# Strassen feed-forward: input tiles of 128 rows, sums on VectorE, five plain blocks, one pair's steps last with second buffers

## The chip, the cores and the metric

The kernel runs on one core of a Trainium2 chip. The metric is the device time of one execution in microseconds (us). TensorE (PE in the profile) multiplies, VectorE (DVE) and ScalarE (ACT) do element-wise work, GpSimd (POOL) too, and SyncE (SP) issues the transfers (DMA). Each engine works through its own queue in order.

## The reference, cut to what matters

One step of an encoder layer for 1104 rows (64 sample rows, 16 meta rows, 1024 prompt rows). The change touches only the first of its two feed-forward blocks:

```python
def half_ffn(x, g, wg, wu, wd):          # x: 1104 x 1024, wg, wu: 1024 x 2816, wd: 2816 x 1024
    h = rmsnorm(x, g)
    return x + 0.5 * ((jax.nn.silu(h @ wg) * (h @ wu)) @ wd)
```

Afterwards come the mixing heads, attention and a second feed-forward block of the same form, which the diff leaves as they are.

## The kernel before

**Numbers.** Every fp32 factor is split into a high part (ScalarE cast to fp32r) and a low part (VectorE: source minus high part), and every product takes three passes on TensorE (`PASSES`, `mm3`): high·high, high·low, low·high.

**Strassen steps.** The 1104 columns of the transposed input are four groups c of F = 276 columns; groups 0 and 1 are pair p = 0, groups 2 and 3 pair p = 1. Of each pair the four quarters (group × upper or lower half of the 1024 features) and sums of them give seven operands, split in `norm_pair`. The 2816 inner columns are 22 blocks j of 128. For a block and a pair, `half_steps` makes gate and up products with seven operand products (`STEPS`) of 12 matmuls, 84 in all; `plain_steps` makes the same without Strassen with 96. Both write the gated result to DRAM (`hd`).

**Weights.** `seq` lists the steps; each step e has a weight set: `half_loads` loads 1 MB in three transfers (`rA` the gate block, `rL` and `rH` the halves of the up block), `half_weights` and `last_weights` form the sums and split them into rings of buffers (`A`, `S`, `T`, `B`). Before, `seq` is 7 blocks for pair 0 alone (two of them plain), the same 7 for pair 1 alone, 13 blocks for both pairs at once (j = 7 to 19), and blocks 20 and 21 for pair 0 and then for pair 1: 31 weight sets. A step for one pair is called a single here, one for both a double. Four sums per Strassen set run on GpSimd (`G.tensor_tensor`); raw buffers `rA`, `rL`, `rT` and split buffers `S`, `T`, `B` exist once, `A` and `rH` twice.

**Input.** `in_rows` brings x in as 12 tiles of 92 rows (three per column group), turns them with TensorE transposes and copies them to `st` and `s` tiles; `norm_pair` scales them; `spill` stores the turned input (`x0`). The vectors of norms and convolutions come in `start2`.

**Down projection.** `down` multiplies with `wd` in groups of two blocks; `down_loads` prepares `wd`, `inner_loads` reads `hd` back and splits it; `x4` are four rows of `x0` for its first residual sums. `first_pair_done` opens their buffers when pair 0 has been used for the last time.

**Order.** A planner (`Tasks`, with the model times of `Clock`) writes out the order of every engine's queue at build time: among tasks whose planned inputs are there, the lowest rank goes first. On the chip the queues then run in this order, whatever arrives late. All DMA of this stage go through SP's one queue. All instructions carry line 424 (a helper), so the profile is read by tiles: `bk` is a PSUM bank, `s` and `st` input tiles, `wx`, `wh`, `wl`, `raw` weight buffers, `sn` and `hb` the results on their way out.

Of the kernel before, what the change touches and what calls it, by code (L numbers as in the profile page):

```python
# [17 lines left out]
P = 128  # L18
# [675 lines left out]
FT = [(0, 92), (92, 92), (184, 92)]  # L694
# [24 lines left out]
def in_rows(s, c, gi, src, xr, dst, ss, fl, rank, before=(), after=()):  # L719

    nc, T = s.nc, s.tasks
    lo, n = FT[gi]
    yield (0, *before)
    xr = xr().rearrange("p k t -> p (k t)")[:, :DM]
    for r0, nr, ap in src:
        nc.sync.dma_start(xr[r0:r0 + nr], ap)
    yield (nc.lag(xr), *after)

    def squares(out):
        nc.scalar.activation(out[:n], xr[:n], AF.Square, accum_out=ss[:n, 3 * (c % 2) + gi:3 * (c % 2) + gi + 1])  # L730
        fl.add((c, gi), nc.complete(ss))
    if c < 2:
        squares(s.waste)
    for h in range(2):
        yield 0, "b"
        b = grab(s)
        for k in range(4):
            nc.tensor.transpose(b[:, k * P:k * P + n], xr[:n, (4 * h + k) * P:(4 * h + k + 1) * P], s.ident[:n, :n])
        T.add(in_out(s, dst(h)[:, :, lo:lo + n], b, n, h, lambda h=h: fl.add((c, gi, h))), rank)
    if c > 1:  # L740
        yield
        squares(xr)
    fl.add(("xr", c, gi))


def in_out(s, dst, b, n, h, done):
    nc = s.nc
    (nc.scalar.copy if h else nc.vector.tensor_copy)(dst, b.rearrange("p (k t) -> p k t", k=4)[:, :, :n])
# [6 lines left out]
def norm_pair(s, p, ss, src, x, raw, more, gain, wk, waits, ready, spill):  # L755
# [3 lines left out]
    V, G = nc.vector, nc.gpsimd  # L759
    raws = None  # L760

    def low(eng, i, src, tile=None):
        x.low(eng, i, src, tile)
        ready.add((p, i), nc.complete(x.l[i]))
    for i in (0, 1):
# [3 lines left out]
        rsqrt(s, wk, r, ss[:, 3 * i:3 * i + 3], P, 3, 1.0 / DM, EPS)  # L769
# [6 lines left out]
        for gi, (lo, n) in enumerate(FT):  # L776
            nc.tensor.matmul(rb[:, lo:lo + n], s.ones, dg[:, gi, :n], start=True, stop=True)
# [3 lines left out]
        for h in (0, 1):  # L781
# [14 lines left out]
    X3, X4 = x.new(13), x.new(5)  # L796
# [32 lines left out]


# [10 lines left out]

def half_weights(s, seq, rings, raw, W):

    nc, T = s.nc, s.tasks
    V, G, A = nc.vector, nc.gpsimd, nc.scalar

    def split(names, srcs, dst, raws):
        h, l = dst
        for i, (n, x) in enumerate(zip(names, srcs)):
            A.copy(h[:, 512 * i:512 * i + 512], x)  # L850
        yield nc.lag(h)
        for i, (n, x) in enumerate(zip(names, srcs)):
            o = slice(512 * i, 512 * i + 512)
            V.tensor_tensor(l[:, o], x, f32(h[:, o]), ALU.subtract)
            W[e, n] = h[:, o], l[:, o]
        T.free(*raws)
    for e in (0, 1):
        to = rings["ST"[e]]
# [14 lines left out]
    for e in range(2, len(seq)):  # L873
# [4 lines left out]
        G.tensor_tensor(t0, a0, b0, ALU.subtract)  # L878
# [5 lines left out]
        G.tensor_tensor(b0, b0, b1, ALU.add)  # L884
# [4 lines left out]
        G.tensor_tensor(a0, b0, a0, ALU.subtract)  # L889
        yield nc.lag(a0), "S"  # L890
        yield from split(("S0", "S1"), (b0, a0), rings["S"].take(), ("rL",))
        G.tensor_tensor(a1, a1, a0, ALU.subtract)
        yield nc.lag(a1), "T"
        yield from split(("T0", "T1"), (t0, a1), rings["T"].take(), ("rT", "rA"))


def last_weights(s, seq, rings, raw, W):

    nc, T = s.nc, s.tasks
    for e in range(2, len(seq)):  # L900
# [9 lines left out]
def plain_steps(s, js, W, x, ready, tmp, hd, done):  # L910
# [22 lines left out]
    for c in (0, 1):  # L933
        for e in (0, 1):
            bs = []
            for n in "AB":
                yield 0, "b", nc.when(W, (e, n))
                b = grab(s)
                for k in range(8):
                    op = (0, 1, 7, 2)[2 * c + k // 4]  # L940
                    if k % 4 == 0:
                        yield 0, ready.wait((0, op))
                    mm3(nc, b[:, :F], [w[:, k * P:k * P + P] for w in W[e, n]], (x.h[op][:, k % 4, :], x.l[op][:, k % 4, :]), k == 0, k == 7)
                bs.append(b)
                if n == "A":
                    T.add(gated(e, c, bs), -1)
            if c:
                T.free("A", "ST"[e])


def half_steps(s, seq, W, x, ready, tmp, hd, done, hooks):
# [25 lines left out]
    for e, (j, ps) in list(enumerate(seq))[2:]:  # L977
        bs, sn, hbs, fl = {}, {}, {}, Flags()
        for name, op, i, bk in STEPS:
# [31 lines left out]
            if op in last:  # L1011
                T.free(last[op])
# [4 lines left out]
def down_loads(s, wd, slots, W):  # L1017

    nc, T = s.nc, s.tasks
    raws = []  # L1020
# [6 lines left out]
    yield from load(0)  # L1027
    for j in range(NF):
        if j + 1 < NF:
# [9 lines left out]
        T.free("raw")  # L1039
# [1172 lines left out]
def layer_kernel(tc, cst, x_prompt, x_sample, cache_mla_ckv, cache_mla_krope, state_gdn, state_conv, meta,  # L2212
# [21 lines left out]
    with ExitStack() as ctx:  # L2234
# [46 lines left out]
        ss = [wk.tile([P, 6], F32, name=f"ss{p}") for p in (0, 1)]  # L2281
        for x in ss:
            nc.vector.memset(x, 1.0)
# [4 lines left out]
        def half_of(c, h):  # L2288
            if c < 2:
                return stage[c][:, 4 * h:4 * h + 4, :]  # L2290
            if (c, h) not in staged:
                staged[c, h] = x01[1].new({(2, 0): 9, (2, 1): 10, (3, 0): 12, (3, 1): 13}[c, h])
            return staged[c, h]

        def rows_of(o, n):
            out = []
            for a, b, ap in ((0, NS, x_sample[0]), (NS, NS + NM, meta), (NS + NM, T_, x_prompt[0])):
                lo, hi = max(a, o), min(b, o + n)
                if lo < hi:
                    out.append((lo - o, hi - lo, ap[lo - a:hi - a, :]))  # L2300
            return out
        xr = [2, 3, 4, 5, 6, 8, 11]
        for c in range(4):
            for gi, (o, n) in enumerate(FT):
                i = 3 * c + gi
                T.add(in_rows(s, c, gi, rows_of(F * c + o, n), lambda i=i: x01[1].new(xr[i % 7]), lambda h, c=c: half_of(c, h), ss[c // 2], tin, -4 if c < 2 else 8,
                              (tin.wait(("xr", (i - 7) // 3, (i - 7) % 3)),) if i > 6 else (), (n1.wait((0, 0)),) if c > 1 else ()), -3 if c < 1 else -1.5 if c < 2 else 10 + i)

        def there(c, h=None):
            return tin.wait(*[(c, gi) if h is None else (c, gi, h) for gi in range(3)])  # L2310
# [47 lines left out]
        state_px, x4 = {}, []  # L2358
# [260 lines left out]
```

## Time and profile before

| | us |
|---|---|
| median of 3 runs | 2513.24 (2512.9 to 2514.95) |
| profiled execution | 2513.59 |
| its span | 2511.8 |
| PE busy in the span | 2379.2 (95%) |
| DVE, ACT, POOL busy | 1371.3, 824.3, 453.7 |

The span is what the trace covers; 1.8 us of the execution lie outside it. Forty slices of the span show PE at 5 to 8 tenths in the first slices and at 9 or more in nearly all the others. Busy PE is modelled, and matmuls overlap, so the mean duration of one matmul is longer than the distance between two of them.

### The profile page before, as it was taken

The page shows a single profiled execution, that of the slowest core. Times are in us where ns is not written, and L with a number is a line of the kernel's source. Part 1 is how long each engine was busy: PE and PEld are TensorE (multiplying, and loading weights), DVE is VectorE, ACT ScalarE, POOL GpSimd, SP SyncE. Part 2 cuts the span into 40 slices and gives each one's busy share as a digit, 9 for nine tenths or more (in the row PEclk, how much of TensorE's full clock was granted, in tenths as well). Part 3 has the DMA queues.
Part 4 walks back from the last instruction along what each step waited for, and adds up shares of the span by engine and source line. Part 5 has one row for each costly group of instructions (what it writes and reads, how often), then busy time and mean ns, then how long its engine had stood idle before and what let it go on. Part 6 is the DMA issues. An engine that isn't in the chain of part 4 may idle for free.

```text
span 2511.8 us, 39219 instructions
## 1 busy us (share of the span) xinstructions
PE 2379.2 (95%) x15552; PEld 2344.1 (93%) x15552; DVE 1371.3 (55%) x3105; ACT 824.3 (33%) x1847; POOL 453.7 (18%) x679
## 2 busy tenths in 40 slices
PE   5868999998999999989998999999999999999999
PEld 5767999998999989989998999999999999999998
DVE  3776644445666666778877656634333333233335
ACT  4343433333111245455543555423111111111113
POOL 0454422222000041332236200221000000000002
PEclk6889999999999999999998999999999999999999
DMA  4323322226322133111122102621111111111011
GB/s 139 105 69 92 97 74 78 78 77 207 120 88 96 39 103 95 37 55 45 53 63 73 53 15 76 209 59 54 48 34 34 51 51 51 42 43 43 27 41 72
DMA packets 210944, 181.28 MB, mean 72 GB/s; under 512 B 12748, under 2 KB 192120, under 8 KB 210632
## 3 DMA queue, kind: packets, MB, share of 16 engines
q1 hardware_dynamic: 210744, 178.77, 23.3%
q8 instruction: 122, 2.00, 0.3%
q14 instruction: 62, 0.51, 0.1%
q10 hardware_dynamic: 16, 0.00, 0.0%
HBM read 143.14 MB, written 35.60 MB: 71 GB/s over the span
## 4 chain that ended last, share of the span: by engine, by line
PE 77%; DVE 9%; DMA 5%; POOL 3%; issue 3%; ACT 2%; SPq 1%; DVEq 0%; POOLq 0%; ACTq 0%
PE bk L424 77%; DMA raw<-in_ffn_wu_dram 2%; DVE wl L424 1%; DMA wx<-in_ffn_wg_dram 1%; DVE cv L424 1%; DVE s L424 1%; POOL raw L424 1%; ACT wh L424 1%; DVE wx L424 1%; SPq L424 1%; DVE rs_q L424 1%; DMA raw<-in_w_out_dram 1%; DMA s<-in_x_prompt_dram 1%; DVE rs_r L424 0%; POOL wx L424 0%
## 5 line engine op out<-in xcount | busy, mean ns | idle before, releaser
L424 PE MATMUL bk<-XH,wh 128*128 128x384 f32 (+1 forms) x1264 | 354.4, 341 | 0.0
L424 PE MATMUL bk<-XL,wh 128*128 128x384 f32 (+1 forms) x1264 | 349.2, 337 | 1.4 <-POOL XL L424 0.8
L424 PE MATMUL bk<-XH,wl 128*128 128x384 f32 (+1 forms) x1264 | 348.5, 336 | 0.0
L424 ACT CAST wh<-raw 128x1024 fp32r<-128x1024 f32 (+5 forms) x124 | 115.0, 928 | 661.4 <-PE bk L424 601.0
L424 PE MATMUL bk<-s,wh 128*128 128x276 f32 x1440 | 290.6, 299 | 18.4 <-ACT sn L424 9.2
L424 DVE TENSOR_TENSOR wl<-raw,wh 128x1024 fp32r<-128x1024 f32 (+5 forms) x124 | 143.2, 1156 | 228.2 <-ACT wh L424 228.0
L424 PEld LDWEIGHTS bk<-s,wh 128*128 128x128 f32 x1440 | 237.9, 197 | 21.4 <-ACT wh L424 10.8
L424 PE MATMUL bk<-s,wx 128*128 128x276 f32 x1560 | 217.3, 296 | 24.7 <-ACT sn L424 14.3
L424 PEld LDWEIGHTS bk<-s,wx 128*128 128x128 f32 x1560 | 208.0, 193 | 27.5 <-ACT sn L424 16.0
L424 PE MATMUL bk<-s,wl 128*128 128x276 f32 x720 | 215.9, 300 | 14.3 <-DVE wl L424 14.2
L424 PEld LDWEIGHTS bk<-XL,wh 128*128 128x128 f32 x1264 | 225.4, 189 | 3.0 <-POOL XL L424 1.7
L424 PEld LDWEIGHTS bk<-XH,wh 128*128 128x128 f32 x1264 | 225.8, 189 | 0.0
L424 PEld LDWEIGHTS bk<-XH,wl 128*128 128x128 f32 x1264 | 225.5, 189 | 0.0
L424 DVE SCALAR_TENSOR_TENSOR X<-bk,X 128x384 f32<-128x384 f32 (+1 forms) x264 | 127.4, 534 | 106.6 <-PE bk L424 106.5
L424 DVE SCALAR_TENSOR_TENSOR R<-bk,R 128x384 f32<-128x384 f32 (+1 forms) x252 | 121.2, 532 | 68.2 <-PE bk L424 68.1
L424 PEld LDWEIGHTS bk<-s,wl 128*128 128x128 f32 x720 | 141.5, 197 | 17.2 <-DVE wl L424 16.9
L424 POOL TENSOR_SCALAR XG<-X,vec 128x384 f32<-128x384 f32 x8 | 10.9, 1367 | 755.8 <-DVE X L424 755.7
L424 DVE TENSOR_TENSOR wl<-wx,wh 128x1024 fp32r<-128x1024 f32 (+1 forms) x60 | 92.4, 1540 | 88.1 <-ACT wh L424 86.7
L424 PE MATMUL bk<-cTh,wh 128*128 128x336 f32 x416 | 134.1, 322 | 0.9 <-ACT cTh L424 0.9
L424 PE MATMUL bk<-cTl,wh 128*128 128x336 f32 x416 | 132.9, 319 | 1.6 <-POOL cTl L424 1.2
L424 PE MATMUL bk<-cTh,wl 128*128 128x336 f32 x416 | 132.6, 319 | 0.0
L424 DVE TENSOR_TENSOR sn<-bk,sn 128x276 f32<-128x276 f32 x126 | 55.7, 442 | 132.8 <-PE bk L424 103.5
(401 smaller groups left out, 4980.8 us busy)
## 6 DMA issues: line engine op xcount, KB each, us to landing
raw<-in_ffn_wd_dram SPq DMA_DIRECT2D x44, 512.0 KB
wx<-in_ffn_wg_dram SPq DMA_DIRECT2D x31, 512.0 KB
raw<-in_ffn_wu_dram SPq DMA_DIRECT2D x62, 256.0 KB
hd<-hb SPq DMA_DIRECT2D x44, 276.0 KB
raw<-in_ffn_wg_dram SPq DMA_DIRECT2D x22, 512.0 KB
raw<-in_ffn_wu_dram SPq DMA_DIRECT2D x22, 512.0 KB
raw<-in_w_in_dram SPq DMA_DIRECT2D x16, 512.0 KB
raw<-in_w_out_dram SPq DMA_DIRECT2D x16, 512.0 KB
```

What stands on the lines that cost most here:

```text
L424: r = f(*args, **kw)
```

## The change

- The input comes in 9 tiles: 80 rows (64 and 16), then eight of 128. A tile that lies across two column groups is copied out in two pieces (`pieces`). Squares, sums and flags go by tile.
- The four sums per weight set, and the sums and low parts in `norm_pair` that were on GpSimd, are on VectorE.
- Blocks 0 to 4 of pair 0 are plain (`NPL = 5`); then 17 doubles (j = 5 to 21); then blocks 0 to 4 of pair 1 as singles: 27 weight sets.
- When the last double has been planned, its pair's space gives second buffers to `rA`, `rL`, `T` and `rT` (`Ring.more`). The `T` split is a task of its own (`third_weights`).
- The first two `wd` blocks are loaded during the singles into extra tiles (`wd2`), the reading of `hd` starts during them too, and the buffers for the first five `wd` blocks come free with the last single alone (names with `!`).

The diff, cut to its core:

```diff
-def in_rows(s, c, gi, src, xr, dst, ss, fl, rank, before=(), after=()):
+def in_rows(s, t, src, xr, dst, ss, fl, rank, before=(), after=()):
...
+        to = [(dst(c, h)[:, :, lo - F * c:hi - F * c], lo - o, hi - o) for c in range(4) for i, lo, hi in pieces(c) if i == t]
+        T.add(in_out(s, to, b, h, lambda h=h: fl.add((t, h))), rank)
...
-                low(G if p and h else V, op, dst, more and op == 7 and more(1))
+                low(op, dst, more and op == 7 and more(1))
...
-    G.tensor_tensor(X4, B22, X3, ALU.subtract)
-    V.tensor_tensor(B11, B22, B12, ALU.subtract)
-    G.tensor_tensor(B12, B21, X4, ALU.subtract)
     yield nc.lag(X3)
+    V.tensor_tensor(X4, B22, X3, ALU.subtract)
...
+    V.tensor_tensor(B12, B22, B12, ALU.subtract)
+    V.tensor_tensor(B11, B21, X4, ALU.subtract)
...
+    yield 0, free
+    x.high(nc, 6, B11)
...
+    def more(self, tile):
+        T = self.s.tasks
+        self.tiles.append(tile)
+        self.n = 1
+        T.caps[self.name] += 1
+        T.idle[self.name].append(T.clock.at["tensor"])
...
-    for e in range(2, len(seq)):
+    for e in range(NPL, len(seq)):
         yield 0, "rT", nc.when(raw, (e, "rA")), nc.when(raw, (e, "rL"))
...
-        G.tensor_tensor(t0, a0, b0, ALU.subtract)
+        V.tensor_tensor(t0, a0, b0, ALU.subtract)
...
-        G.tensor_tensor(b0, b0, b1, ALU.add)
+        V.tensor_tensor(b0, b0, b1, ALU.add)
...
-        G.tensor_tensor(a0, b0, a0, ALU.subtract)
+        V.tensor_tensor(a0, b0, a0, ALU.subtract)
...
-        G.tensor_tensor(a1, a1, a0, ALU.subtract)
-        yield nc.lag(a1), "T"
-        yield from split(("T0", "T1"), (t0, a1), rings["T"].take(), ("rT", "rA"))
+        V.tensor_tensor(a1, a1, a0, ALU.subtract)
+        raw[e, "T"] = t0, a1
+def third_weights(s, seq, rings, raw, W):
+    for e in range(NPL, len(seq)):
+        yield 0, "T", s.nc.when(raw, (e, "T"))
+        yield from split_weights(s, W, e, ("T0", "T1"), raw[e, "T"], rings["T"].take(), ("rT", "rA"))
...
-    for c in (0, 1):
-        for e in (0, 1):
+    for c, e in [(0, 0), (0, 1), (1, 0), (1, 1)] + [(c, e) for e in range(2, NPL) for c in (0, 1)]:
...
-        seq = [(j, [0]) for j in range(7)] + [(j, [1]) for j in range(7)] + [(j, [0, 1]) for j in range(7, NF - 2)] + [(j, [p]) for p in (0, 1) for j in (NF - 2, NF - 1)]
+        seq = [(j, [0]) for j in range(NPL)] + [(j, [0, 1]) for j in range(NPL, NF)] + [(j, [1]) for j in range(NPL)]
...
         def first_pair_done():
             right.close(1)
             px = state_px[0] = right("xpA")
+            xt = right("xt")
+            for n, w in (("rA", 1024), ("rL", 512)):
+                rings[n].more(xt.tile([P, w], F32, name=f"{n}2"))
+            t = [big(px, f"X{x}0", CH[0][1], F32R if x == "H" else F32).rearrange("p k t -> p (k t)") for x in "HL"]
+            rings["T"].more((t[0][:, :1024], t[0][:, 1024:2048]))
+            rings["rT"].more(t[1][:, :512])
+            T.add(early(px, xt), -2)
+        def early(px, xt):
+            yield 0, lambda: 0.0 if (E - NPL + 1, "S0") in W1 else None
             T.add(inner_loads(s, hd, lambda g: pairs(big(px, ("XH1", "XL1")[g % 2], CH[1][1], F32)), inner_slots, done, hs), -2)
+            for i in (0, 1):
+                yield 0, lambda: 0.0 if (E - NPL + 1 + i, "B1") in W1 else None
+                t = xt.tile([P, 1024], F32, name=f"r{i}")
+                nc.sync.dma_start(t, ffn1_wd[0, i * P:(i + 1) * P, :])
+                wd2.append(t)
...
+            T.add(down_loads(s, ffn1_wd[0], slots, Wd, wd2), -2)
...
-            yield from half_steps(s, seq, W1, x01, n1, wk, hd, done, {E - 3: first_pair_done})
+            yield from half_steps(s, seq, W1, x01, n1, wk, hd, done, {E - NPL - 1: first_pair_done, E - 2: lambda: state.add("last step", nc.at["tensor"])})
+            yield 0, lambda: 0.0 if 1 in Wd else None
```

## Rows read from the trace of the kernel before

**Rows 1.** Stages: window, us, each engine's busy us (instructions), PE clock, DMA share, GB/s.
```profile
0.00:57.17 57.17, 28.33 (x179) 25.80 (x179) 20.45 (x59) 23.01 (x41) 0.20 (x4) 0.69 0.39 125
57.17:84.20 27.03, 27.03 (x196) 27.03 (x196) 18.88 (x23) 10.37 (x17) 10.69 (x4) 0.90 0.40 111
84.20:150.00 65.80, 41.47 (x244) 39.16 (x243) 50.80 (x81) 22.53 (x37) 29.06 (x15) 0.75 0.32 95
150.00:280.60 130.60, 106.74 (x748) 101.87 (x748) 80.39 (x101) 53.06 (x102) 57.38 (x37) 0.94 0.33 95
280.60:558.73 278.13, 278.13 (x2186) 278.13 (x2187) 137.46 (x212) 99.77 (x212) 87.91 (x56) 1.00 0.25 76
558.73:619.44 60.71, 51.53 (x373) 49.99 (x373) 33.19 (x48) 24.44 (x45) 18.67 (x12) 0.92 0.56 186
619.44:632.92 13.48, 9.61 (x58) 9.31 (x56) 4.17 (x8) 2.09 (x2) 0.00 (x0) 0.98 0.71 267
632.92:881.00 248.08, 247.95 (x1476) 247.66 (x1477) 168.99 (x295) 47.66 (x54) 2.93 (x3) 0.99 0.27 86
881.00:2511.80 1630.80, 1588.43 (x10106) 1565.16 (x10104) 857.00 (x2284) 541.36 (x1341) 246.83 (x550) 0.98 0.19 58
```

**Rows 2.** The same view, 4 us stretches; in the first only 92-row input tiles arrive.
```profile
24.00:28.00 4.00, 1.56 (x10) 1.29 (x10) 0.54 (x1) 1.62 (x3) 0.00 (x0) 0.62 0.26 105
...
60.00:64.00 4.00, 4.00 (x25) 4.00 (x24) 0.00 (x0) 0.42 (x2) 0.17 (x1) 0.69 1.13 305
```

**Rows 3.** Timeline of the input stage: start us, us, engine, operation [idle before <-releaser].
```profile
5.46 1.06 ACT L424 ACTIVATE s<-s 92x1024 f32<-92x1024 f32 x1 [3.24 <-DMA s<-in_x_prompt_dram]
...
28.11 1.46 PE L424 MATMUL bk<-ident,s 92*128 92x92 f32 x8 [2.05 <-DMA s<-in_x_prompt_dram]
...
39.34 1.31 DVE L424 TENSOR_TENSOR s<-s,s 128x1104 fp32r<-128x1104 f32 x1 [0.28 <-ACT s L424]
...
57.17 0.81 PE L424 MATMUL bk<-s,wh 128*128 128x276 f32 x2
```

**Rows 4.** Timeline, two 512 KB loads of `wd` (128 rows) issued together at 610.46.
```profile
614.01 1.05 ACT L424 CAST wh<-raw 128x1024 fp32r<-128x1024 f32 x1
...
616.19 1.05 ACT L424 CAST wh<-raw 128x1024 fp32r<-128x1024 f32 x1
```

**Rows 5.** Groups by form, 57 to 150 us: busy us, mean ns of one | idle before.
```profile
L424 DVE TENSOR_TENSOR s<-s,s 128x1104 fp32r<-128x1104 f32 x8 | 15.5, 1942 | 3.2 <-ACT s L424 3.2
...
L424 DVE TENSOR_TENSOR wl<-wx,wh 128x1024 fp32r<-128x1024 f32 x3 | 7.1, 2372 | 2.1 <-ACT wh L424 2.1
...
L424 DVE SCALAR_TENSOR_TENSOR s<-bk,vec,st 128x276 f32<-128x276 f32 x8 | 3.5, 495 | 6.1 <-PE bk L424 6.1
```

**Rows 6.** Groups by form where POOL stands still: 0 to 57 us, last row 609 to 619.5.
```profile
L424 DVE TENSOR_TENSOR s<-s,s 128x1104 fp32r<-128x1104 f32 x2 | 2.6, 1308 | 1.5 <-ACT s L424 1.5
L424 DVE TENSOR_TENSOR wl<-wx,wh 128x1024 fp32r<-128x1024 f32 x2 | 2.5, 1225 | 5.4 <-ACT wh L424 5.4
...
L424 DVE TENSOR_TENSOR wx<-raw,wx 128x512 fp32r<-128x512 f32 x2 | 1.4, 684 | 0.0
```

**Rows 7.** Groups by form, 0 to 560 us: one of POOL's four sums.
```profile
L424 POOL TENSOR_TENSOR raw<-raw 128x512 f32<-128x512 f32 x26 | 52.7, 2028 | 2.9 <-DMA raw<-in_ffn_wu_dram 1.0
```

**Rows 8.** Timeline of one single: a weight set is asked for, its first sum, the next set asked for.
```profile
204.93 0.37 SPq L424 DMA_DIRECT2D wx<-in_ffn_wg_dram  x1
...
210.10 1.28 POOL L424 TENSOR_TENSOR raw<-wx,raw 128x512 f32<-128x512 f32 x1 [6.96 <-DMA raw<-in_ffn_wu_dram]
...
218.56 0.37 SPq L424 DMA_DIRECT2D wx<-in_ffn_wg_dram  x1
```

**Rows 9.** Doubles, 280 to 559 us: timeline, groups by form, waits (us, times, longest).
```profile
309.76 2.25 DVE L424 TENSOR_TENSOR wl<-wx,wh 128x1024 fp32r<-128x1024 f32 x1 [5.04 <-ACT wh L424]
...
L424 DVE TENSOR_TENSOR sn<-bk,sn 128x276 f32<-128x276 f32 x79 | 35.0, 443 | 78.1 <-PE bk L424 73.6 <-ACT sn L424 4.5
...
POOL raw L424 <- DMA raw<-in_ffn_wu_dram: 186.9, 15, 15.0
```

More of the change, by code (lines that the diff above doesn't have):

```diff
@@ L693, with pieces @@
 F = 276
-FT = [(0, 92), (92, 92), (184, 92)]
+NPL = 5
+def pieces(c):
+    return [(t, max(TT[t][0], F * c), min(sum(TT[t]), F * c + F)) for t in (2 * c, 2 * c + 1, 2 * c + 2)]
 STEPS = (("P1", "A0", 0, "B"), ("P5", "S0", 3, "D"), ("P6", "S1", 4, "B"), ("P3", "T1", 2, "D"),
@@ L752, in in_out, with norm_pair, low @@
     yield
-def norm_pair(s, p, ss, src, x, raw, more, gain, wk, waits, ready, spill):
+def norm_pair(s, p, ss, src, x, raw, more, gain, wk, waits, ready, spill, free):
     nc, T = s.nc, s.tasks
-    V, G = nc.vector, nc.gpsimd
+    V = nc.vector
     raws = None
-    def low(eng, i, src, tile=None):
-        x.low(eng, i, src, tile)
+    def low(i, src, tile=None):
+        x.low(V, i, src, tile)
         ready.add((p, i), nc.complete(x.l[i]))
@@ L775, in norm_pair @@
         rb = grab(s)
-        for gi, (lo, n) in enumerate(FT):
-            nc.tensor.matmul(rb[:, lo:lo + n], s.ones, dg[:, gi, :n], start=True, stop=True)
+        for gi, (t, lo, hi) in enumerate(pieces(c)):
+            o, n = TT[t]
+            nc.tensor.matmul(rb[:, lo - F * c:hi - F * c], s.ones[:n], dg[:n, gi, lo - o:hi - o], start=True, stop=True)
         if p:
@@ L839, in half_loads, with split_weights @@
             raw[e, n] = t
+def split_weights(s, W, e, names, srcs, dst, raws):
+    nc = s.nc
+    h, l = dst
+    for i, x in enumerate(srcs):
+        nc.scalar.copy(h[:, 512 * i:512 * i + 512], x)
+    yield nc.lag(h)
+    for i, (n, x) in enumerate(zip(names, srcs)):
+        o = slice(512 * i, 512 * i + 512)
+        nc.vector.tensor_tensor(l[:, o], x, f32(h[:, o]), ALU.subtract)
+        W[e, n] = h[:, o], l[:, o]
+    s.tasks.free(*raws)
 def half_weights(s, seq, rings, raw, W):
     nc, T = s.nc, s.tasks
[L845 to L856, printed above, removed]
-    for e in (0, 1):
-        to = rings["ST"[e]]
+    V, A = nc.vector, nc.scalar
+    for e in range(NPL):
+        to = rings["TS"[e % 2]]
         yield 0, to.name, nc.when(raw, (e, "rA"))
@@ L1011, in half_steps, with down_loads @@
             if op in last:
-                T.free(last[op])
+                T.free(last[op] + "!" * (e == len(seq) - 1))
         if e in hooks:
             hooks[e]()
-def down_loads(s, wd, slots, W):
+def down_loads(s, wd, slots, W, raws):
     nc, T = s.nc, s.tasks
-    raws = []
+    n = len(raws)
     def load(j):
@@ L1026, in load @@
         nc.sync.dma_start(raws[-1], wd[j * P:(j + 1) * P, :])
-    yield from load(0)
     for j in range(NF):
-        if j + 1 < NF:
+        if n <= j + 1 < NF:
             yield from load(j + 1)
@@ L1038, in down_loads @@
         W[j] = tuple(t.rearrange("p (k n) -> p k n", n=P) for t in (h, l))
-        T.free("raw")
+        if j >= n:
+            T.free("raw")
 def inner_loads(s, hd, raw, slots, done, hs):
@@ L2280, in layer_kernel @@
         stage = [stg.tile([P, 8, F], F32, tag=f"st{c}", name=f"st{c}") for c in (0, 1)]
[L2281 to L2283 removed]
+        ss = wk.tile([P, 9], F32, name="ss")
+        nc.vector.memset(ss, 1.0)
         x0 = s.dram.tile([8, P, T_], F32, name="x0")
```

124 lines of the change are left out of this document (55 added, 69 removed).

## The prediction

> **What bounds the kernel now.** I read the busy time of the engines by stage first, then the timelines of the stages in which TensorE stands still, then the groups by form for what one instruction costs. From 632.92 on PE is busy all the time in the down projection (247.95 of 248.08 us) and nearly so afterwards (1588 of 1631) [rows 1]; nothing there is edited. The doubles, 280.60 to 558.73, are full too: 278.13 us for 13 steps of 168 matmuls, 2184, which is 127.35 ns per matmul at clock 1.00. That is my price of PE work in this stage. All that can be won lies in four other windows [rows 1]:
>
> - 0 to 57.17, no product yet: the input arrives.
> - 57.17 to 84.20, two plain blocks: 192 matmuls, 24.45 us at the price, measured 27.03; clock 0.90. The 2.6 us are the half clock of the first microseconds.
> - 84.20 to 280.60, twelve singles, 1008 matmuls, worth 128.4 us and lasting 196.4: 68 us lost, at clock 0.75 and 0.94.
> - 558.73 to 632.92: about 13 us lost by the last four singles, and 3.9 in the first steps of down (9.61 busy of 13.48), which wait for `wd`.
>
> By matmuls: 2 plain blocks and 42 Strassen blocks are 192 + 42·84 = 3720, worth 473.7 us; they lie between 57.17 and 619.44, 562.3 us. So 88.6 us of that stretch, 3.9 behind it, and a good part of the 57 ahead of it are waits. PE is the bound of the whole, but here it waits for others.
>
> **Input.** A 92-row tile arrives at 105 GB/s and a DMA share of 0.26, about 4 of 16 engines [rows 2]. The share follows from a rule of the Trainium skill, "DMA: Bandwidth & Descriptors", section "Why a DMA increments its semaphore by 16 and not by 1": a transfer is spread over the largest number up to 16 that divides its slowest dimension, so 4 for 92 and 16 for 128; the 0.26 agrees. No input load of 128 rows is in the trace, but `wd` blocks are such loads: two issued together are cast at 614.01 and 616.19, so 2.18 us for the second 512 KB, 240 GB/s [rows 4]; the busiest stretch shows 305 GB/s [rows 2]. SP's order stays: three tiles, the first weight set (1 MB), then the other tiles. Tile 0 is there by 5.46 [rows 3]; after it come 2 tiles, 1 MB and 2 tiles of pair 0, six times 512 KB, 13.1 us: 18.5. Before, pair 0's last tile was there at 28.11 and its first two operands were split at 40.65, 12.5 us later [rows 3], so now at 31. PE's queue holds the transposes of pair 1's four tiles and of the vectors ahead of the first plain product: that is why it starts only at 57.17 although its operands stood at 40.65. Four tiles more land at 18.5 + 8.7 = 27.2, and their transposes at half clock take 4·1.46 = 5.8 [rows 3], then the vectors, 1 us: 34. I take 34 for the first plain product; 29 with 305 GB/s, 57 if nothing changes. By the page's ceiling of 435 GB/s the 13.1 us would be 7.2, an estimate, and the total about 2414; the row of a real load is what I use.
>
> **PE work.** 5 plain and 39 Strassen blocks are 480 + 3276 = 3756 matmuls, 36 more than before, 478.3 us (+4.6). Twenty-four transposes fewer lie before the start and are in its time. The slow first microseconds stay: 2.6.
>
> **Plain blocks and the way into the doubles.** A plain block needs one weight set per 12.2 us of PE instead of 10.7, no sums, and on DVE 1.23 + 2·0.68 for its low parts and 2·0.44 for its results [rows 6, 9], 3.5 us, where a Strassen single needs 1.23 + 5·0.68 + 5·0.44 = 6.8. So 61 us of plain work give DVE time for the second pair. It needs it. From 34 us on DVE owes: pair 0's second group and sums, 8 scalings (0.495 in the mean [rows 5]) and 2 + 8 passes of 1.31 [rows 6] and 3 us of small ones, about 20 us; pair 1: 16 scalings, 11 passes, small ones and copies, about 30; weight sets 1 to 4 of the plain blocks 10.4; results 4.4; the first double's set 1.23 + 5·0.68 and four sums of 0.68, 7.4. Together 72 us, in 61 us of plain products and about 18 of the first double, whose operands are needed one after another. That closes at 91% of DVE, and part of the order is a chain with ScalarE, so I expect PE to wait: 3 us in the plain blocks (0 to 8) and 7 at the entry (0 to 30: 30 if DVE's share stays at the 77% that it had from 84 to 150 [rows 1], which makes 93 us of 72, plus the time that the chain waits behind PE's queue).
>
> A rule of the skill speaks against this step: "Perfetto Trace Analysis", section "Optimizing Scalar/DVE Operations", says that a saturated DVE may hand work to ScalarE or even GpSimd; this change hands it back. The same paragraph adds that DVE and GpSimd share an SBUF port, so that moving between these two may not help. The rows show the second part: while POOL works, a pass of 1104 takes DVE 1.94 us and a low part of 1024 takes 2.37 [rows 5]; while it stands still they take 1.31 and 1.23 [rows 6]. POOL needs up to 2.03 us for a sum of 512 [rows 7], DVE 0.68 for the like [rows 6]. Four sums on DVE cost 2.7 us per set, and the contention that goes away gives back 1.0 on the 1024 low part alone.
>
> **Doubles.** 17 instead of 13, inside the 478.3. DVE's load per double was 137.46/13 = 10.6 us [rows 1]; now 1.23 + 5·0.68 + 2.7 + 10·0.44 = 11.7 of 21.4. Cover is ample: no loss. What is new is that DVE's queue, not POOL's, waits for the raw weights to land. Behind it stand the `sn` additions that empty the banks. But DVE stood there anyway: the low part of the gate block waited 5.04 us for a cast that waited for the same load, and PE missed nothing [rows 9].
>
> **Singles at the end.** Before, one single's set took 218.56 − 204.93 = 13.6 us from load to load: 5.2 until the first sum, then POOL's sums and the splits [rows 8]. PE needs 10.7. With two raw buffers the 5.2 overlap, and four sums take 2.7 instead of about 6.6. The rings `S` and `B` stay single, but `S` is free after three of seven products, and has 7.6 us for 2.7 of work and ScalarE's casts. DVE has 6.8 + 2.7 = 9.5 us per single and another 5 for `hd` and `wd` in all, 52 in 53.5, less what the last double prepares: tight. I take 4 us (0 to 15, the old period).
>
> **Into down.** `hd` of blocks 0 and 1 is finished by the second single, three singles ahead; `wd` 0 and 1 are loaded and split during the singles. 1 us (0 to 13.5, the old window). SP gets these loads in front of the last `hd` store; all weight loads are planned ahead of them. Four weight sets fewer save 4 MB of transfers that are hidden now; I give them nothing.
>
> **Sum.** 34 + 478.3 + 2.6 + 3 + 7 + 4 + 1 = 529.9 until down runs, against 619.44 + 3.87 = 623.3: 93.4 us less. The profiled execution is 2513.59 (span 2511.8 and 1.8 outside it, 0.35 above the median): 2420. The order behind 881 is planned anew from a shifted clock, and 42 us of it are PE waits [rows 1]; I take 0 there, and 4 to each side.
>
> **Rivals.** (1) DVE bounds the second pair: 30 us at the entry instead of 7, 2443. For it: 77% DVE from 84 to 150 while PE waited. Against it: about a quarter of that was contention. (2) The singles keep their period and down its wait: 5·2.9 + 13.5 instead of 5, 2443. For it: one `S` and one `B`. (3) Larger tiles bring nothing, products start at 57: 2443. For it: SP's one queue, in which 1 MB of weights stands in the middle. Against it: share 0.26. (4) Slower than before: DVE's head of queue waits for raw weights in every double, and PE with it. POOL waited 186.9/15 = 12.5 us per set at this place [rows 9]; if the sum stands as early in DVE's queue, DVE is held 7.4 us beyond the 5.04 that did no harm, and 17·7.4 = 126 us make 2546. It decides from 93/17 = 5.5 us per double. Against it: the planner puts the sum after the planned landing, and evacuations fill the time. (5) The second buffers and early loads do nothing and DVE gives back what plain blocks win, so that about nothing moves: three of the other rivals and more at once.
>
> **Chances.** Forecast 73%, (1) 10, (2) 7, (3) 5, (4) 4, (5) 1. The forecast's own bounds: 29 us start and no waits give 2400, with the rest of the kernel 2396; start 38, waits 8, 15, 12 and 5 give 2449. Any one of the first three rivals alone lies below 2450. I set 2396 to 2450. A measurement of this kernel can tell about 0.2%, 5 us, from no change: faster 0.95, same 0.01, slower 0.04.
>
> **What would show it.** DMA share near 1 during the input and a first plain product near 34; no POOL busy before 500 us, low parts of 1024 at 1.23; doubles at 21.4 us; singles at 10.7 to 11.5; the first down product near 530. I am wrong if plain blocks wait for DVE's low parts for more than 15 us, if PE waits inside doubles, or if a stage behind down loses more than 5 us.

## The result and the profile after

The changed kernel takes 2413.35 us in the median of 4 runs (2411.2 to 2418.12); the kernel before took 2513.52 on the same chip (2512.9 to 2514.95). The ratio is 0.9603, with a 95% interval of 0.9587 to 0.962. The profiled execution took 2413.15 us, its span 2411.3, 100.5 us less than before.

I cut the trace at three points that each kernel has: the first plain product (`bk<-s,wh`), the first down product, and the mixing norm behind the down projection (`dg` on DVE). This is the stage view of the kernel before at these cuts, with the columns of [rows 1]:

```profile
57.17:619.44 562.27, 504.90 (x3741) 496.18 (x3741) 320.71 (x463) 210.17 (x412) 203.72 (x122) 0.94 0.32 96
619.44:886.33 266.89, 262.89 (x1565) 262.30 (x1564) 177.65 (x311) 52.55 (x61) 6.88 (x17) 0.99 0.30 99
886.33:2511.80 1625.47, 1583.10 (x10075) 1559.83 (x10073) 852.51 (x2274) 538.55 (x1335) 242.88 (x537) 0.98 0.19 58
```

And of the kernel after, where the first product stands at 24.55, the doubles from 109.86 to 462.00, and the down projection begins at 518.19:

```profile
0.00:24.55 24.55, 22.55 (x160) 21.68 (x161) 14.43 (x42) 14.07 (x25) 0.20 (x4) 1.00 0.82 267
24.55:109.86 85.31, 78.87 (x607) 77.37 (x608) 65.24 (x124) 38.88 (x61) 0.00 (x0) 1.00 0.45 135
109.86:462.00 352.14, 352.14 (x2763) 352.14 (x2764) 180.28 (x336) 131.02 (x262) 0.00 (x0) 1.00 0.25 76
462.00:518.19 56.19, 52.21 (x407) 51.55 (x406) 41.13 (x71) 28.36 (x54) 0.00 (x0) 1.00 0.49 159
518.19:789.40 271.21, 264.28 (x1565) 263.14 (x1564) 179.90 (x313) 53.07 (x63) 6.88 (x17) 0.98 0.32 110
789.40:2411.30 1621.90, 1577.21 (x10075) 1554.40 (x10073) 854.29 (x2274) 538.11 (x1335) 241.75 (x537) 0.98 0.19 58
```

The start gives 57.17 − 24.55 = 32.6 us; first product to down gives 562.27 − 493.64 = 68.6; the way to the norm costs 4.3; the rest gives 3.6. The 68.6 has two halves. PE's idle time there falls from 57.4 to 10.4 us, so 47 are waits. The other 22 are busy time. Before, 3720 matmuls were busy for 504.9 us, 31 more than 3720 · 127.35 ns, at a granted clock of 0.94 in the mean; now 3756 are busy for 483.2, 5 more than the price, at 1.00. Most of these 26 us are the clock: counted in the two traces, 193 products of this stretch had the next one start 0.23 us behind them in the kernel before, and 13 in the kernel after, where the distance at clock 1.00 is 0.127; that alone is 19 us. The rest was not told apart. So the kernel before lost, beside 57 us of waits, 31 us in the stretches between them, some 20 of it in slower matmuls, and the change gives most of both back.

All profiles at the same three cuts, in us (each span in one execution; "PE waits" are those of the second column's stretch as the waits view names them):

| kernel | first product | to down (PE waits) | down to norm | rest | span |
|---|---|---|---|---|---|
| before | 57.17 | 562.27 (57.2) | 266.89 | 1625.47 | 2511.8 |
| after | 24.55 | 493.64 (10.8) | 271.21 | 1621.90 | 2411.3 |
| x_92_36 | 48.34 | 498.89 (12.4) | 269.69 | 1619.68 | 2436.6 |
| x_96_32 | 27.40 | 495.27 (9.0) | 271.32 | 1624.81 | 2418.8 |
| sums_pool | 23.97 | 490.75 (6.0) | 264.05 | 1623.43 | 2402.2 |
| norm_pool | 23.99 | 497.13 (10.5) | 270.58 | 1626.60 | 2418.3 |
| no_second | 23.56 | 516.50 (20.7) | 260.97 | 1627.27 | 2428.3 |
| no_second_pool | 24.22 | 500.17 (13.6) | 261.10 | 1625.41 | 2410.9 |
| singles_mid | 23.73 | 537.92 (40.1) | 263.43 | 1625.32 | 2450.4 |
| npl3 | 24.33 | 511.88 (27.5) | 266.47 | 1621.02 | 2423.7 |
| npl7 | 24.31 | 494.46 (7.9) | 265.94 | 1619.49 | 2404.2 |
| hd_first | 23.74 | 493.31 (10.2) | 268.56 | 1625.29 | 2410.9 |
| wd_first | 23.74 | 495.14 (9.2) | 261.45 | 1625.57 | 2405.9 |
| best1 | 23.85 | 490.22 (5.4) | 261.82 | 1624.31 | 2400.2 |

No kernel edits what lies behind the norm, and still that column goes from 1619.5 to 1627.3. It is planned anew each time, and executions of one kernel differ too, by 11.4 us in norm_pool (2408.94 to 2420.37); which of the two it is was not told apart. A difference of a few us in the whole time may come from there; a stage's own column tells more. That column moves by itself as well: hd_first and wd_first edit nothing ahead of down and show 493.31 and 495.14 there.

### The profile page after: what moved, and what is told of

It is laid out like the page before. It is cut to its first block, busy times and chain, and to the rows that moved or that the text cites. A ratio compares the mean times of both kernels' runs of the same rounds, so it can differ in the third digit from the quotient of the medians.

```text
span 2411.3 us, 39048 instructions
## 1 busy us (share of the span) xinstructions
PE 2347.2 (97%) x15570; PEld 2320.3 (96%) x15570; DVE 1335.3 (55%) x3156; ACT 803.5 (33%) x1799; POOL 248.8 (10%) x557
## 4 chain that ended last, share of the span: by engine, by line
PE 85%; DVE 8%; DMA 2%; issue 2%; ACT 2%; POOL 1%; SPq 0%; DVEq 0%; POOLq 0%; ACTq 0%
PE bk L424 85%; DVE s L424 1%; DVE cv L424 1%; DMA raw<-in_ffn_wu_dram 1%; DVE wl L424 1%; DVE rs_q L424 1%; DVE rs_r L424 0%; POOL rs_q L424 0%; DVE st L424 0%; ACT s L424 0%; DMA raw<-in_ffn_wd_dram 0%; ACT wh L424 0%; POOL XL L424 0%; POOL tkq L424 0%; DMA wx<-in_ffn_wg_dram 0%
## 5 line engine op out<-in xcount | busy, mean ns | idle before, releaser
L424 ACT CAST wh<-raw 128x1024 fp32r<-128x1024 f32 (+4 forms) x115 | 108.6, 946 | 610.5 <-PE bk L424 573.0
L424 PE MATMUL bk<-s,wh 128*128 128x276 f32 x1472 | 284.1, 291 | 4.9 <-ACT sn L424 2.2
L424 DVE TENSOR_TENSOR wl<-raw,wh 128x1024 fp32r<-128x1024 f32 (+4 forms) x115 | 127.4, 1109 | 216.5 <-ACT wh L424 216.5
L424 PEld LDWEIGHTS bk<-s,wh 128*128 128x128 f32 x1472 | 232.3, 188 | 6.1 <-ACT sn L424 2.5
L424 PE MATMUL bk<-s,wx 128*128 128x276 f32 x1476 | 196.6, 290 | 1.8 <-DVE s L424 1.8
L424 PEld LDWEIGHTS bk<-s,wx 128*128 128x128 f32 x1476 | 191.3, 188 | 2.0 <-DVE s L424 2.0
L424 PE MATMUL bk<-hh,wdh 128*128 128x336 f32 (+1 forms) x528 | 122.6, 330 | 0.0
L424 PE MATMUL bk<-hh,wdl 128*128 128x336 f32 (+1 forms) x528 | 122.0, 329 | 0.0
L424 PE MATMUL bk<-hl,wdh 128*128 128x336 f32 (+1 forms) x528 | 121.8, 329 | 0.0
```

What stands on the lines that cost most here:

```text
L424: r = f(*args, **kw)
```

## The experiments

Each is an edit of the changed kernel. None leaves out a part of the computation. The early `wd` loads and the separate `T` split were not taken back by themselves, so no run shows what each of them is worth.

### The input's transfers: x_92_36 and x_96_32

The theory is that the 92-row transfers are slow because of their row count; the rival is that the number of tiles, and of transposes with them, sets the start. The first kernel keeps the new tiles and loads each in two pieces, the second in two pieces of another size.

```diff
-        return [(0, P, x_prompt[0, P * (t - 1):P * t, :])]
+        return [(0, 92, x_prompt[0, P * (t - 1):P * (t - 1) + 92, :]), (92, P - 92, x_prompt[0, P * (t - 1) + 92:P * t, :])]
```

(x_96_32 has 96 in place of 92.)

> The changed kernel with one edit: each input tile of 128 rows is loaded by two transfers, of 92 and of 36 rows, instead of one; tiles, transposes and copies stay nine. Theory (the spread of a load over the DMA engines sets the first product): a 92-row part takes about 3.6 us as before the change, the 36 rows some 0.5 more, so nine tiles and 1 MB of weights take 5.5 + 8*4.1 + 3 = 41 us; the first plain product moves from 24.55 to 40-45 us and the time from 2413 to 2428-2436. Rival (fewer tiles, fewer transposes and waits are what brings the early start): first product at 25-28 us, 2410-2417.

Measured: 2439.36, ratio 0.972 (0.9701 to 0.9738), a little more than was expected, as is the first product at 48.34.

> The same edit with parts of 96 and 32 rows: as many transfers as with 92 and 36 rows. Theory (spread): both parts spread like 128 rows, so the first product stays at 24-27 us and the time at 2411-2417. Rival (the number of transfers or their size is what costs): like the kernel with 92 and 36 rows, 2428 or more.

Measured: 2421.9, ratio 0.9645 (0.9627 to 0.9664), between the theory's window and the rival's.

Input stretches of 4 us (columns as in [rows 1]), first of the kernel after:

```profile
8.00:12.00 4.00, 4.00 (x27) 4.00 (x26) 2.32 (x11) 3.36 (x8) 0.00 (x0) 1.00 1.16 327
12.00:16.00 4.00, 4.00 (x39) 4.00 (x37) 3.90 (x11) 3.00 (x7) 0.00 (x0) 1.00 1.03 411
16.00:20.00 4.00, 4.00 (x39) 4.00 (x37) 2.70 (x7) 2.45 (x5) 0.00 (x0) 1.00 1.06 369
```

then of x_92_36:

```profile
24.00:28.00 4.00, 1.59 (x15) 1.43 (x14) 2.46 (x6) 1.57 (x4) 0.00 (x0) 0.99 0.35 125
28.00:32.00 4.00, 4.00 (x24) 4.00 (x22) 0.76 (x2) 1.23 (x4) 0.00 (x0) 0.58 0.34 126
```

With the same tiles, squares and transposes, the rate is 125 GB/s where it was 327 to 411, the DMA share a third where it was over 1, and the first product moves from 24.55 to 48.34. PE falls idle on the way (1.59 of 4 us), and its clock to 0.58 behind that. x_96_32 moves as many pieces and starts at 27.40, 2.9 us late. The split by itself costs these 2.9; the other 20.9 us belong to the row counts 92 and 36. So the row count is the cause of most of the gain at the start. It need not be all: with nine tiles x_92_36 still starts 8.8 us ahead of the kernel before (57.17), and it has fewer tiles and also fewer loads of 92 rows, eight instead of eleven; these were not told apart. (Of the 7.5 us by which x_96_32's span is longer, 2.9 lie at the start, 1.7 ahead of the norm and 2.9 behind it.)

### The sums of a weight set: sums_pool, no_second, no_second_pool

The first puts the four sums back on POOL (the first piece of the diff, one sum of four), the second takes the second buffers away (the second piece), the third does both.

```diff
-        V.tensor_tensor(t0, a0, b0, ALU.subtract)
+        nc.gpsimd.tensor_tensor(t0, a0, b0, ALU.subtract)
...
-            for n, w in (("rA", 1024), ("rL", 512)):
-                rings[n].more(xt.tile([P, w], F32, name=f"{n}2"))
-            t = [big(px, f"X{x}0", CH[0][1], F32R if x == "H" else F32).rearrange("p k t -> p (k t)") for x in "HL"]
-            rings["T"].more((t[0][:, :1024], t[0][:, 1024:2048]))
-            rings["rT"].more(t[1][:, :512])
```

> The changed kernel with the four sums of each weight set back on GpSimd; the sums of norm_pair stay on VectorE. Theory: in the doubles it costs nothing (VectorE is half idle), though VectorE's low part of 1024 columns goes from 1.22 to about 2.2 us; at the entry to the doubles and in the last singles, where VectorE is 70 to 85% busy, the contention and the longer chain cost 3 to 8 us each: 2418-2428. Rival A (all hidden since the second buffers): 2410-2416. Rival B (sums on VectorE are themselves what makes PE wait at the entry): 2405-2411.

Measured: 2404.12, ratio 0.9573 (0.9553 to 0.9594). The theory fell: I had expected a loss. But only 2.9 of the 9.1 us by which its span is shorter lie in the stretch where the sums are; 7.2 lie between down and norm, and the section on the way into down says why.

> The changed kernel without second buffers for rA, rL, T and rT; order and everything else stay. Theory (the last singles keep up because load and work overlap): with one buffer each, load, sums and splits follow one another, 5 us and 8 to 9 us, so a single takes 13.5-14.5 us instead of 11 and the time is 2424-2430. Rival (shorter sums on VectorE suffice, buffers matter little): singles at 11-11.5 us, 2412-2416.

Measured: 2429.67, ratio 0.9671 (0.9657 to 0.9685). The time lies in the theory's window.

> The changed kernel without second buffers and with the four weight sums back on GpSimd. Theory (with single buffers the sums stand in a chain load - sums - splits - load, so their place counts; with second buffers it is hidden): four sums of 1.3-2.0 us instead of 0.68 lengthen each of the last singles by 3-5 us against no_second (2429.7), 2438-2450, while with second buffers the move to GpSimd made the kernel faster. Rival (sums on GpSimd are better in any case, because VectorE is relieved): 2418-2426.

Measured: 2413.08, ratio 0.9608 (0.9592 to 0.9623). Here too the theory fell, and the rival gained more than it had asked for.

The contention that I had priced is there. The groups by form from the first product to down (busy us, mean ns of one, idle before), of the kernel after:

```profile
L424 DVE TENSOR_TENSOR wl<-wx,wh 128x1024 fp32r<-128x1024 f32 x24 | 29.2, 1218 | 3.5 <-ACT wh L424 3.5
L424 DVE TENSOR_TENSOR raw<-wx,raw 128x512 f32<-128x512 f32 x20 | 13.8, 692 | 83.8 <-DMA raw<-in_ffn_wu_dram 83.8
```

and of sums_pool:

```profile
L424 DVE TENSOR_TENSOR wl<-wx,wh 128x1024 fp32r<-128x1024 f32 x24 | 45.3, 1887 | 86.7 <-ACT wh L424 85.6 <-PE bk L424 1.2
L424 POOL TENSOR_TENSOR raw<-wx,raw 128x512 f32<-128x512 f32 x20 | 27.2, 1358 | 340.1 <-DMA raw<-in_ffn_wu_dram 340.1
```

A low part of 1024 costs DVE 1.89 us beside POOL's sums, 1.22 without. What I had not priced stands in the last field of the two `raw<-wx,raw` rows: at the first sum of a set DVE's queue waits for the load, 83.8 us for the 20 of them. In POOL's queue only the other sums stand behind it, and 340.1 us of it, much as before the change (336.1), go with fewer waits of PE. In DVE's queue the additions that empty PE's banks stand behind it. In the timeline of no_second (columns as in [rows 3]):

```profile
478.05 0.38 SPq L424 DMA_DIRECT2D wx<-in_ffn_wg_dram  x1
...
482.95 0.69 DVE L424 TENSOR_TENSOR raw<-wx,raw 128x512 f32<-128x512 f32 x1 [4.93 <-DMA raw<-in_ffn_wu_dram]
...
484.99 0.69 DVE L424 TENSOR_TENSOR raw<-raw 128x512 f32<-128x512 f32 x1 [1.35 <-DMA raw<-in_ffn_wu_dram]
486.74 0.79 DVE L424 TENSOR_TENSOR sn<-bk,sn 128x276 f32<-128x276 f32 x2
...
487.58 3.13 PE L424 MATMUL bk<-s,wx 128*128 128x276 f32 x12 [4.90 <-DVE sn L424]
...
496.94 0.38 SPq L424 DMA_DIRECT2D wx<-in_ffn_wg_dram  x1
```

DVE is held for 4.93 and 1.35 us, and only then come the additions `sn` that empty PE's banks; PE stands still for 4.90 us until they have. A set takes 496.94 − 478.05 = 18.9 us, the next one 19.0. With the sums on POOL the same loads stand 14.0 apart, the next ones 14.8:

```profile
472.14 0.38 SPq L424 DMA_DIRECT2D wx<-in_ffn_wg_dram  x1
...
486.17 0.38 SPq L424 DMA_DIRECT2D wx<-in_ffn_wg_dram  x1
```

Of PE's waits the view of 460 us to down in no_second names this (engine, line, releaser: us, times, longest); in no_second_pool no wait of PE for DVE's `sn` is named, and POOL waits instead (450 to 510 us):

```profile
PE bk L424 <- DVE sn L424: 8.3, 2, 4.9
```

```profile
POOL raw L424 <- DMA raw<-in_ffn_wu_dram: 39.9, 5, 14.6
```

So with single buffers the sums on DVE cost 516.50 − 500.17 = 16.3 us to down, and the intervals of the two times lie apart. With second buffers the sets are loaded earlier, and 493.64 − 490.75 = 2.9 are left, little more than the 1.8 between hd_first and wd_first, which edit nothing there. The singles then fill PE for 54.02 of 54.72 us in sums_pool, against 52.21 of 56.19 in the kernel after. The second buffers are worth 516.50 − 493.64 = 22.9 us on this stretch with the sums on DVE, and 9.4 with them on POOL: much of their work is to hide the wait that the other part of the change brought. This is the mechanism of the prediction's rival (4), in the singles. In the doubles it does no harm: PE is busy for 352.14 of 352.14 us.

A rule of the Trainium skill, "Perfetto Trace Analysis", section "Optimizing Scalar/DVE Operations", had spoken against this step: a saturated DVE may hand work even to GpSimd. The runs come out the way of that rule, but not by its condition: DVE is busy for 41.13 of 56.19 us in the singles of the kernel after. What the timeline of no_second shows is not a full engine but the order of its queue.

### The passes of the norm: norm_pool

```diff
-    V.tensor_tensor(X4, B22, X3, ALU.subtract)
+    nc.gpsimd.tensor_tensor(X4, B22, X3, ALU.subtract)
...
-    V.tensor_tensor(B11, B21, X4, ALU.subtract)
+    nc.gpsimd.tensor_tensor(B11, B21, X4, ALU.subtract)
...
-        x.low(V, i, src, tile)
+        x.low(nc.gpsimd if p and i in (1, 2) else V, i, src, tile)
```

> The changed kernel with the norm_pair work that was on GpSimd before put back there: two subtractions per pair and two low parts of pair 1; the weight sums stay on VectorE. Theory (GpSimd passes of 1104 take about 3.5 us, they stand one behind the other in the chain of pair operands and slow VectorE down beside them): the entry to the doubles waits 4-10 us more, 2416-2423. Rival (as with the weight sums: what is taken off VectorE is worth more than the contention): 2405-2412.

Measured: 2419.43, ratio 0.9625 (0.96 to 0.965), an interval that overlaps that of the kernel after. To down it takes 497.13 against 493.64, 3.5 us more; 4.7 more lie behind the norm, where nothing was edited, and 1.2 come back elsewhere. The time is the expected one, but the theory's mechanism is not seen: from 24 to 112 us, where the entry to the doubles is, PE waits 6.5 us as against 6.8, and the singles, which the edit doesn't touch, are where it lost. So whether this step is worth anything stays open.

### How many plain blocks, and where the singles stand: npl3, npl7, singles_mid

```diff
-NPL = 5
+NPL = 3
```

(7 in npl7). singles_mid does the singles of pair 1 before the doubles. The space of the second buffers is then not yet free, so it has none, and no_second is what it is to be compared with.

```diff
-        seq = [(j, [0]) for j in range(NPL)] + [(j, [0, 1]) for j in range(NPL, NF)] + [(j, [1]) for j in range(NPL)]
+        seq = [(j, [0]) for j in range(NPL)] + [(j, [1]) for j in range(NPL)] + [(j, [0, 1]) for j in range(NPL, NF)]
```

> The changed kernel with three plain blocks instead of five (and so three singles at the end, 19 doubles). 24 matmuls fewer are worth 3 us, two singles fewer about 1. Theory (plain blocks cover the making of pair 1's operands on VectorE, which ends near 105 us whatever PE does): PE stands at the entry for 15-24 us more, 2424-2433. Rival (VectorE's work shrinks with the blocks, PE waits little): 2407-2412.

Measured: 2423.37, ratio 0.9646 (0.963 to 0.9661), a little under what was expected.

> The changed kernel with seven plain blocks (seven singles at the end, 15 doubles). 24 matmuls more cost 3.1 us. Theory (five already cover VectorE's work: PE waits only about 2 us at the entry): 2414-2420, of which up to 2 us more from singles. Rival (VectorE still is short at the entry with five): 2407-2412.

Measured: 2408.73, ratio 0.9588 (0.9571 to 0.9606). The time lies in the rival's window, and the interval overlaps that of the kernel after.

> The changed kernel with the five singles of pair 1 put between the plain blocks and the doubles (and without second buffers, which have no space there). Theory: these singles then need pair 1's operands in 10.7 us instead of 21.4 per step while VectorE is still making them, and weights at single rate without second buffers (13.5-14.5 us per step); PE waits 15-30 us there; the way into down is no longer prepared during singles but stays covered in part: 2430-2455. Rival (where the singles stand is of no matter, only input and second buffers are): about as without second buffers, 2424-2430.

Measured: 2452.78, ratio 0.9763 (0.9745 to 0.978).

With three plain blocks PE reaches the doubles before pair 1 is split (`dg` holds the norm's factors of a column group). From the timeline of npl3:

```profile
80.98 1.65 PE L424 MATMUL bk<-dg,ones 128*128 128x20 f32 x6 [7.53 <-DVE dg L424]
...
90.97 0.60 PE L424 MATMUL bk<-s,wh 128*128 128x276 f32 x1 [8.34 <-ACT s L424]
...
536.21 1.99 PE L424 MATMUL bk<-st,wh 128*128 128x336 f32 x4 [6.57 <-ACT st L424]
```

The third row is the first down product, which comes behind three singles here. At the first two places the kernel after waits 2.3 and 1.1 us (the waits view, 24 to 112 us):

```profile
PE bk L424 <- DVE s L424: 3.2, 3, 1.8
PE bk L424 <- DVE dg L424: 2.3, 1, 2.3
PE bk L424 <- ACT s L424: 1.1, 1, 1.1
```

Two plain blocks more than three give 511.88 − 493.64 = 18.2 us to down, though they add 24 matmuls (3.1 us). PE's waits from 24 to 112 us, where pair 1 is split, fall from 20.6 to 6.8 us; the 6.57 us ahead of the first down product are the way into down, not this cover. Two more than five add 24 again and 0.8 us: the 2.9 that they take off PE's waits nearly pay for them. So from five to seven this stage is flat. That npl7's span is still 7.1 shorter comes from the way into down (5.3) and from behind the norm (2.4), which is not what either side had argued. singles_mid loses 537.92 − 516.50 = 21.4 us to no_second: as many singles, at the place where DVE and ScalarE also split pair 1, and PE waits 40.1 us instead of 20.7. But 12.4 of the 40.1 stand ahead of the first down product:

```profile
561.65 1.89 PE L424 MATMUL bk<-st,wh 128*128 128x336 f32 x5 [12.39 <-ACT wh L424]
```

In singles_mid the loads for down begin only behind the last weight set, at 547.77 us. So the place of the singles is a part of the gain of its own, but the larger part of it is the way into down, and 7 to 9 us are left for the rest, the splitting of pair 1 among it.

### The way into down: hd_first, wd_first, best1

In the kernel after, PE stands still for 6.67 us behind its first products of down (`R` are the additions that empty the banks here):

```profile
515.35 1.34 SPq L424 DMA_DIRECT2D XH<-x  x2
516.73 0.43 SPq L424 DMA_DIRECT2D raw<-in_ffn_wd_dram  x1
...
524.42 1.04 ACT L424 CAST wx<-raw 128x1024 fp32r<-128x1024 f32 x1 [8.60 <-DMA raw<-in_ffn_wd_dram]
525.70 1.09 ACT L424 CAST st<-XH 128x1104 fp32r<-128x1104 f32 x1
...
526.85 1.29 PE L424 MATMUL bk<-st,wh 128*128 128x336 f32 x3 [6.67 <-ACT st L424]
```

The load of the third `wd` block is issued behind the 1.1 MB of `XH<-x`, and its cast waits for it for 8.60 us at the head of ScalarE's queue. The cast that PE needs, `st<-XH`, has its data and stands behind it. hd_first holds the `wd` cast back until the second `hd` split is queued:

```diff
-def down_loads(s, wd, slots, W, raws):
+def down_loads(s, wd, slots, W, raws, hs):
...
-        yield nc.lag(raws[j]), name
+        yield nc.lag(raws[j]), name, lambda: 0.0 if j != n or 1 in hs else None
```

wd_first also issues these loads ahead of `XH<-x`:

```diff
+            T.add(down_loads(s, ffn1_wd[0], slots, Wd, wd2, hs), -2)
             for x in "LH":
-                yield 0, lambda: 0.0 if x == "L" and (E - 2, "T1") in W1 else state.get("last step")
+                yield 0, lambda: 0.0 if x == "L" and (E - 2, "T1") in W1 else state.get("last step") if len(wd2) > 3 else None
...
-            T.add(down_loads(s, ffn1_wd[0], slots, Wd, wd2), -2)
```

> The changed kernel with one edit: the cast of wd block 2 is planned only after both blocks of the first hd group are split, so that ScalarE's queue does not stand before that load. Theory (the 6.7 us wait after the first down product is a head-of-queue wait on ScalarE): it goes, down runs through from 518 us, 2404-2408. Rival (the loads of this moment are simply late, at 330 GB/s, and the wait moves to the second group): 2411-2416.

Measured: 2413.56, ratio 0.9616 (0.9595 to 0.9638). The theory fell; the rival held.

> The changed kernel with two edits at the way into down: as in hd_first, and the two rows of x0 for m = 2, 3 are loaded only after wd blocks 2 and 3. Theory (what is left of the wait in hd_first is the late wd blocks behind 1.1 MB of x0, which hold VectorE's queue before the residual sums): down from its first product to the mixing norm takes 262-265 us instead of 271.2 and the time is 2403-2408. Rival (the loads together are the limit; the sums for m = 2, 3 now wait for x0): 267-270 us, 2409-2413.

Measured: 2406.66, ratio 0.9581 (0.956 to 0.9603).

In hd_first the wait only changes its queue:

```profile
522.14 1.05 ACT L424 CAST wx<-raw 128x1024 fp32r<-128x1024 f32 x1 [4.16 <-DMA raw<-in_ffn_wd_dram]
523.22 1.23 DVE L424 TENSOR_TENSOR wx<-raw,wx 128x1024 fp32r<-128x1024 f32 x1 [3.90 <-ACT wx L424]
...
526.92 0.95 PE L424 MATMUL bk<-st,wh 128*128 128x384 f32 x4 [2.90 <-DVE R L424]
...
539.84 0.94 PE L424 MATMUL bk<-st,wh 128*128 128x384 f32 x4 [2.01 <-DVE R L424]
```

Now DVE's low part of the late block waits at the head of DVE's queue, and the additions `R` are behind it; PE's waits there are 4.9 us instead of 6.9. With the load itself earlier, 271.21 us become 261.45, and PE has no wait there at all. In wd_first the load leaves at 508.95, ahead of `XH<-x` and 9.9 us before the first down product, where it was 1.5 us before it in the kernel after:

```profile
508.95 0.33 SPq L424 DMA_DIRECT2D raw<-in_ffn_wd_dram  x1
```

So the cause was the time at which the load leaves SP's queue. The whole times of wd_first and the kernel after do not tell it by themselves, since their intervals overlap. sums_pool, which edits nothing here, agrees: by its planned order this load leaves 8.5 us before the first down product (514.72), and the way to the norm takes 264.05.

```profile
506.20 0.81 SPq L424 DMA_DIRECT2D raw<-in_ffn_wd_dram  x1
```

> The changed kernel with weight sums on GpSimd (as in sums_pool) and both edits of wd_first. Theory (two separate gains, VectorE's queue in the singles and the loads before down): 2400-2405, at or a little under sums_pool (2404.1), since there the wait before down was already small. Rival (the gain of sums_pool before down was chance of the planned order and is undone by the edits): 2406-2412.

best1 is wd_first with the sums of sums_pool. Measured: 2402.46 (2396.64 to 2403.2), ratio 0.9561 (0.9539 to 0.9583). It beats both kernels; its interval lies just below that of the kernel after. To down it takes 490.22, to the norm 261.82. It is not told from sums_pool (2404.12, intervals overlap): the two gains do not add up, since most of what sums_pool gained was the early `wd` load that both have.

## Why the prediction was right, point by point

The forecast was 2420, the time 2413.35, inside the range, and the gain came where the forecast had put it: at the start, in the waits of PE up to down, and not behind it. The terms, against the profile:

- **Start: 34 forecast, 24.55 measured, and below the low bound of 29.** The term that was mis-sized is the rate. I took 240 GB/s from two `wd` loads [rows 4], the input came at 327 to 411. The row was misread: neither of its two casts waited for a load, and between them ScalarE waited for DVE, so their distance of 2.18 us is not the time of the second load. In the timeline of the kernel before, and in its stage view at that place:

```profile
615.64 0.43 ACT L424 ACTIVATE sn<-sn 128x276 f32<-128x276 f32 x1 [0.58 <-DVE sn L424]
```

```profile
612.00:614.00 2.00, 2.00 (x17) 2.00 (x17) 0.00 (x0) 0.73 (x2) 0.00 (x0) 0.99 0.94 295
```

By the ceiling of 435 GB/s that the Trainium skill gives ("DMA: Bandwidth & Descriptors", section "Specifications"), my sum had come to about 2414. That sum put the ceiling on the first six loads alone; on the four behind them too, the start would be 24.3 us and the total 2410, an estimate. The measured rates lie on both sides of the middle between 240 and 435.

- **Why the 92 rows are slow: right.** x_92_36 and x_96_32 show it together. The rule of the Trainium skill, "DMA: Bandwidth & Descriptors", section "Why a DMA increments its semaphore by 16 and not by 1" (4 engines for 92 rows, 16 for 96 and 128), agrees with a share of 0.35 for 92 rows and 36, and of 1.03 and more for 128.
- **Half clock at the start: 2.6 forecast, nothing measured.** PE's clock is 1.00 in every stage up to down; before, it was 0.90 in the first products [rows 1]. The input now follows closely enough to keep PE busy for 22.55 of 24.55 us before it.
- **Matmuls: 478.3 forecast, 483.2 measured** as busy time to down, 5 us more.
- **Plain blocks and entry: 3 + 7 forecast, 6.4 measured** (85.31 − 78.87). npl3 shows that this cover is needed: with two blocks less, PE waits 7.53 and 8.34 us there at single instructions.
- **Doubles: no loss forecast, none measured.** But DVE's queue does wait there, as forecast, without harm to PE.
- **Sums on DVE: called nearly free for what contention gives back; the step that failed.** Contention did shrink, by 0.67 us on a low part of 1024, and the move still gains nothing: without second buffers it loses 16.3 us to down, with them 2.9, which is hardly clear of what the column moves by itself. I weighed durations, but with single buffers the price was a place in a queue. That the 2.9 with second buffers are the same wait is not shown: in the singles of the kernel after no wait of PE names DVE's additions. The longest, 2.23 us, is for ScalarE's `sn`, behind weight casts of which the first had itself waited 4.44 us for a load:

```profile
462.56 1.05 ACT L424 CAST wh<-rA 128x1024 fp32r<-128x1024 f32 x1 [4.44 <-DMA rA<-in_ffn_wg_dram]
...
465.50 0.52 PE L424 MATMUL bk<-s,wh 128*128 128x276 f32 x2 [2.23 <-ACT sn L424]
```

I had seen the mechanism, as rival (4), and had put it in the doubles, where evacuations had time to spare.

- **Singles: 4 forecast, 4.0 measured** (56.19 − 52.21). The waits view names ScalarE's `sn` (2.2 us) and DVE's `XH` (1.8). Without second buffers the period was 18.9 us, longer than the 13.6 of before [rows 8]: rival (2) would have been worse than I priced it.
- **Into down: 1 forecast, about 10 measured** (271.21 against 261.45 in wd_first). I had written that SP gets these loads early and that the weights are planned ahead; true for blocks 0 and 1. Block 2 stood behind `XH<-x`, a queue that I had not walked through.
- **The rest: 0 forecast, −3.6 measured,** inside the 4 that I had given.

The errors add up: −9.4 and −2.6 at the start, 4.9 of matmuls, −3.6 at the entry, 8.8 into down, −3.6 behind the norm; and before lost 1.6 us more into down (266.89 − 261.45) than the 3.87 that I had counted. That makes −7.1, the difference between 93.4 forecast and 100.5 measured. That the total came so near is in part luck: about 21 us of errors to one side stand against 14 to the other.

## What to carry to other kernels

When work is moved to another engine, price the place in that engine's queue, not its duration alone: an instruction that waits for a transfer belongs in a queue where nothing urgent stands behind it, even if that engine is the slower one. Where such a wait must be taken away, look for the transfer that is late and move that, since reordering one queue behind it hands the wait to the next. And count slow matmuls with the waits before them: here 22 of 68.6 us came back as busy time, most of it matmuls that had run at the lower clock.

## What was not expected of the hardware

- Loads of 128 rows of 4 KB each, issued in a row, came at 327 to 411 GB/s over stretches of 4 us; a load of 92 rows and one of 36 in turn came at 125. Splitting each 128-row tile into 96 and 32 rows cost only 2.9 us at the first product.
- The four sums of a set took POOL 2.03, 1.61, 1.36 and 1.33 us in the mean in sums_pool, 6.3 together, against 0.69 each on DVE, and a low part of 1024 on DVE took 1.89 beside them, 1.22 alone. With single buffers the engine that is slower and disturbs the other was still the better place.
- PE's clock fell to 0.58 in the stretch behind an idle one (1.59 of 4 us busy) in x_92_36, and stayed at 1.00 in the kernel after, where PE had been kept busy from the first tiles on.
